# A gate piece moved into the attention, one unit's output products brought forward, and column halves at the end of a hybrid attention step

## The chip, the cores and the metric

The kernel runs on one core of one Trainium2 chip. The metric is the device time of one execution in microseconds (us), lower being better. Of the core's engines this text speaks of PE (TensorE, matrix products), DVE (VectorE), ACT (ScalarE), POOL (GpSimd) and SP (SyncE, which here only issues transfers, in order). Matrix products land in eight accumulation banks of 128 x 512 numbers; each engine works through its own instructions in the order of the program, and every bank or tile that is used again has to be read out first.

## The reference

One layer of a hybrid backbone on 128 context tokens and 1024 latent tokens of width 1024, all in 32-bit floats. The input is normalised and modulated, projected once, and split into queries, keys, values and gates of two mixers of 8 heads (2 key heads each, head width 64). Mixer A attends from every latent token to all 1152 keys, mixer B to a band of 128 to each side and the context keys, with a sink logit; the context tokens attend only to themselves. The outputs, each times the SiLU of its gate, go through one output projection, and are added to the input:

```python
def merge_out(o_a, g_a, o_b, g_b, w_out):
    return jnp.concatenate([o_a * jax.nn.silu(g_a), o_b * jax.nn.silu(g_b)], axis=-1) @ w_out

q_a, k_a, v_a, g_a, q_b, k_b, v_b, g_b = project(h, w_in[l], qn_a[l], kn_a[l], qn_b[l], kn_b[l])
...
o_a = global_attn_latent(q_a, k_a, v_a, cache_k_a[:, l], cache_v_a[:, l])
o_b = window_attn_latent(q_b, k_b, v_b, cache_k_b[:, l], cache_v_b[:, l], sink_b[l])
xs = xs + gate * merge_out(o_a, g_a, o_b, g_b, w_out[l])
```

## The kernel before

Most products are made of two or three: a number is split into a rounded high part and the low part that is left, and high x high, high x low and low x high go into one bank.

**Projections and gates** come first. The last of them are mixer B's gates (`gates`, a generator with one piece per turn): 512 gate columns in four groups `ch` of 128, tokens in three ranges (0 to 512, 512 to 768, 768 to 1152), so twelve pieces. A piece is 24 products into one bank (L259, L263, L264: eight weight slices, three products each; 128 x 384 for the last token range); a step later `put_gates` applies SiLU on ACT (L290, tile `sg`) and sends the result by SP to `g_dram` (`gd`), from which each attention unit loads its gate tile `sgl`. Beside the products of these pieces run the row maxima of attention units 0 and 2 (list `beside`, 26 items, spread evenly) and the splitting of `w_out` into its parts (`WO_STEPS`). Then comes one table load on ACT (L1074): after it exp and log are used, and the SiLU function no more.

**Attention** is a hand-written list of slots over 36 units (token tile t, mixer m, key head g): for t = 1 to 8 in turn (t,A,0), (t,B,0), (t,A,1), (t,B,1), the context tile's four units as the last ones (32 to 35). A unit of mixer A has 9 slots (blocks of 128 keys), one of mixer B 2 or 3, a context unit is padded to 2. Unit 0 has slots 0 to 8, unit 1 slots 9 to 11, unit 2 slots 12 to 20, unit 3 slots 21 to 23, unit 4 begins at 24. One turn of the main loop, one step, does in this order:

- `tick`: whatever earlier steps put off to this one (`later`).
- `scores` of the slot: mixer A: two products into a bank of pair B (L1125 with `qt`, L1126 with `qb`, which holds the negative row maxima; together `st`), exp on ACT (L1128, `pe`), the high part by an ACT cast (L1132, `ph`), the low part on POOL (L1136, on DVE for block 4; `pl`). Mixer B: four transposes of ready weights (L1120), an ACT copy (L1121, `ph`) and a subtraction on DVE a step later (L1122, `pl`).
- what is due at this step (`due`): the maxima of unit i are made during unit i-2 (`max_items`: PE L886 into a bank of pair A, tile `pmx`, DVE reduction L887, 12 each); `finish` closes them at step `start[i-2] + MX_END` = 10, and two steps later a transpose (L905, `ptm`) and a DVE product (L906) fill `qb`. Mixer B's weights (`weight_items`: scores `sn` L943 and L944, the masked minimum on DVE L947) are made in unit i-1.
- output products from the queue `outq`, 2.5 a step.
- `values` of the slot three steps back (LAG): L1146, L1148, L1149 into the unit's bank `pv` of pair C.

After a unit's last values: 1, 4 and 6 steps later (`END_AT`; for the context tile 2, 4, 5) ACT forms the reciprocal row sums from `pv` (`inverse`), DVE writes the quotient into the scratch tile `spare`, columns 768 to 1536, a third for each of three units (`gated`, L1170), POOL multiplies by the gate, and ACT and POOL split the result (`parts`, `ogh` and `ogl`). When a pair of units (A and B of one key head) is done, its 24 output products (`out_items`, `po`, L1217: two column halves n of 512, four slices of 128, three products each) enter `outq`; n = 0 goes to bank D and n = 1 to bank E. With the tile's last product DVE multiplies by the row `gate` (L1223), adds the input (L1224, `yt`) and SP sends the result.

**The last tile** (the context tokens) has its products in this order: two slices for both column halves, then the two other slices for both; at the end its second column half is read in two pieces of 256 columns. `spare` and the `gate` rows lie in tiles of the normalised input that the gates no longer need.

Of the kernel before, what the change touches and what calls it, by code (L numbers as in the profile page):

```python
# [9 lines left out]
F32 = mybir.dt.float32  # L10
# [8 lines left out]
P = 128  # L19
D = 1024  # L20
# [27 lines left out]
MX_END = 10  # L48
SPLIT_LAG = 2
# [32 lines left out]
AHEAD = 3  # L82

# [25 lines left out]
def hybrid_step(ctx, tc, x_prompt, x_sample, cache_k_a, cache_v_a, cache_k_b, cache_v_b,  # L109
# [749 lines left out]

    qp2 = []  # L860
# [194 lines left out]
    beside[:2] = 0.0, (len(beside[2]) + 0.5) / 64  # L1055
# [23 lines left out]
    spare = h_slot(1, 2, 4, "spare").bitcast(F32)  # L1079
    wo_big[2] = h_slot(1, 2, 0, "wo_big2")  # L1080
    gate = spare[:, 0:512], wo_big[2].bitcast(F32)[:, 1024:1536]
    for n in range(2):
        nc.sync.dma_start(gate[n], gate_row[0:1, 512 * n : 512 * n + 512].to_broadcast([P, 512]))
    ogp = ctx.enter_context(tc.tile_pool(name="ogp", bufs=NOG, side="right"))
    w2 = ctx.enter_context(tc.tile_pool(name="w2", bufs=2, side="right"))
    def blocks(t, m, g):
# [117 lines left out]
    def out_items(t, g):  # L1204
# [3 lines left out]
        def mm(n, k, p):  # L1208

            if k == KS[0] and p == 0:  # L1210
                po[n] = bank("DE"[n], f"po{t}_{n}")
# [5 lines left out]
            nc.tensor.matmul(po[n], a, wo_parts[KT * n + k][lo], start=(k == KS[0] and p == 0),  # L1217
                             stop=(k == KS[-1] and p == 2))
            if n == 1 and k % 2 == 1 and p == 2:
                held[0] -= 1  # L1220
            if k == KS[-1] and p == 2:
                for q in (slice(0, 256), slice(256, 512)) if last and n else (slice(0, 512),):
                    nc.vector.tensor_tensor(po[n][:, q], po[n][:, q], gt[n][:, q], op=ALU.mult)  # L1223
                    nc.vector.tensor_tensor(yt[n][:, q], po[n][:, q], yt[n][:, q], op=ALU.add)  # L1224
                    nc.sync.dma_start(y_tile[t][:, 512 * n + q.start : 512 * n + q.stop], yt[n][:, q])

        ks = KS[4 * g : 4 * g + 4]
        return [lambda n=n, k=k, p=p: mm(n, k, p)
# [122 lines left out]
```

## Time and profile before

| | before |
|---|---|
| time, median of 3 runs (lowest to highest) | 711.05 us (710.64 to 711.44) |
| the profiled execution: its time / its span | 710.47 / 708.7 us |
| mean granted PE clock in it | 0.997 |
| PE busy | 690.7 us, 97% |
| DVE busy | 469.8 us, 66% |
| ACT busy | 409.8 us, 58% |
| POOL busy | 335.3 us, 47% |
| read / written in memory | 58.69 / 19.18 MB |

The span is the traced part of one execution, in us from its start; times of the trace are such positions. A row of the timeline gives start, length, engine, line, operation, tiles (out<-in) and their size; a bracket [0.41 <-DVE spare L1170] says that the engine had stood idle for 0.41 us, and that DVE's instruction of line 1170 on `spare` ended this. PE's rows overlap (one begins while the one before drains), so that their price is the distance from start to start. The table of stages gives each engine's busy us and instructions in the order PE, its weight loads, DVE, ACT, POOL, and then the granted clock of PE, the busy share of the transfer engines and GB/s. The attention begins at about 302 us.

### The profile page before, as it was taken

Reading aid. Unit: us, or ns where it says so; the run is one execution under the profiler, and the core shown is the slowest. Engines: PE = TensorE matmul, PEld = TensorE weight load, DVE = VectorE, ACT = ScalarE, POOL = GpSimd, SP = SyncE. Lnnn points to the kernel's source line nnn. Section 1 sums busy time; section 2 is a strip of 40 time slices with the busy share of each in tenths; the row PEclk is TensorE's granted clock in tenths of the full one; section 3 lists DMA queues with packets and bytes.
Section 4 is the critical chain, followed back from the end, with each engine's and each line's share of the span. In section 5 each row is a group of like instructions: output and inputs, shape, how many; then the busy total and the mean of one; then the engine's idle time right before and its main releaser. Section 6 shows DMA issues by size and latency. Waiting matters only on the chain. (4 is left out here: it accounts for less than half of the span.)

```text
span 708.7 us, 10599 instructions
## 1 busy us (share of the span) xinstructions
PE 690.7 (97%) x3508; PEld 557.7 (79%) x3508; DVE 469.8 (66%) x1019; ACT 409.8 (58%) x829; POOL 335.3 (47%) x356
## 2 busy tenths in 40 slices
PE   6999999999999999999999999999999999999987
PEld 3778988878778889966788788888888888787865
DVE  4767257967868855637867578666775776675662
ACT  6646412412413431088777887788778777877760
POOL 4547033233223411256656655665576557555660
PEclk9999999999999999999999999999999999999999
DMA  8962273358353106432222121212221221222323
GB/s 324 414 216 92 78 302 75 89 158 260 104 125 99 46 31 216 130 100 63 73 68 87 48 83 53 73 55 75 68 82 39 79 70 54 74 74 68 104 68 120
DMA packets 53560, 78.58 MB, mean 111 GB/s; under 512 B 7096, under 2 KB 25720, under 8 KB 52608
## 3 DMA queue, kind: packets, MB, share of 16 engines
q1 hardware_dynamic: 45328, 65.96, 27.7%
q10 hardware_dynamic: 8176, 11.94, 6.3%
q8 instruction: 28, 0.46, 0.3%
q14 instruction: 28, 0.23, 0.1%
HBM read 58.69 MB, written 19.18 MB: 110 GB/s over the span
## 5 line engine op out<-in xcount | busy, mean ns | idle before, releaser
L1136 POOL TENSOR_TENSOR pl<-pe,ph 128x512 fp32r<-128x512 f32 x130 | 167.5, 1291 | 144.7 <-DVE nm L947 67.2
L887 DVE TENSOR_REDUCE mx<-pmx 128x1 f32<-128x384 f32 x192 | 101.3, 552 | 57.4 <-PE pmx L886 56.1
L1128 ACT ACTIVATE pe<-st 128x512 f32<-128x512 f32 x146 | 86.8, 594 | 28.0 <-PE st L1126 27.0
L1132 ACT CAST ph<-pe 128x512 fp32r<-128x512 f32 x146 | 90.6, 621 | 4.8
L1146 PE MATMUL pv<-ph,v_hi 128*128 128x512 f32 x208 | 83.5, 401 | 2.2 <-DVE spare L1170 2.2
L1149 PE MATMUL pv<-pl,v_hi 128*128 128x512 f32 x208 | 82.7, 398 | 0.0
L1217 PE MATMUL po<-wo,ogh 128*128 128x512 f32 x216 | 72.5, 394 | 0.2 <-DVE yt L1224 0.2
L174 POOL TENSOR_TENSOR rs_q<-ms_q,mhalf 128x8 f32<-128x8 f32 x18 | 34.1, 1897 | 80.9 <-DVE ms_q L172 80.9
L947 DVE CUSTOM_DVE_ANT_0 sn<-sn,mask,nsink 128x512 f32<-128x512 f32 (+1 forms) x64 | 46.4, 724 | 37.8 <-PE sn L944 36.7
L886 PE MATMUL pmx<-kha,qt 128*128 128x384 f32 x192 | 61.0, 363 | 0.4 <-DVE mx L887 0.2
L1125 PE MATMUL st<-qt,kha 128*128 128x512 f32 x144 | 58.0, 403 | 1.5 <-ACT pe L1128 0.8
L1126 PE MATMUL st<-qb,kla 68*128 68x512 f32 x144 | 57.5, 399 | 1.1 <-DVE qb L906 1.1
L1148 PE MATMUL pv<-ph,v_lo 128*64 128x512 f32 x146 | 57.9, 397 | 0.0
L1149 PEld LDWEIGHTS pv<-pl,v_hi 128*128 128x128 f32 x208 | 39.5, 190 | 16.9 <-POOL pl L1136 0.2
L933 ACT ACTIVATE pen<-sn,nm 128x512 f32<-128x512 f32 (+2 forms) x72 | 45.0, 626 | 6.5 <-DVE nm L947 3.1
L1121 ACT CAST ph<-st 128x512 fp32r<-128x512 f32 x62 | 36.4, 586 | 19.9 <-PE st L1120 18.2
L1146 PEld LDWEIGHTS pv<-ph,v_hi 128*128 128x128 f32 x208 | 39.3, 189 | 10.5 <-ACT ogh L1182 2.4
L1217 PEld LDWEIGHTS po<-wo,ogh 128*128 128x128 f32 x216 | 40.1, 188 | 6.8 <-DVE yt L1224 0.6
L646 ACT CAST qo0q<-ptq 128x512 fp32r<-128x512 f32 x18 | 10.6, 586 | 58.0 <-PE ptq L643 56.7
L1122 DVE TENSOR_TENSOR pl<-st,ph 128x512 fp32r<-128x512 f32 x62 | 42.5, 686 | 2.2 <-ACT ph L1121 1.5
L1217 PE MATMUL po<-wo,ogl 128*128 128x512 f32 x108 | 42.5, 394 | 0.0
L886 PEld LDWEIGHTS pmx<-kha,qt 128*128 128x128 f32 x192 | 35.5, 190 | 6.2 <-DVE mx L887 1.2
(213 smaller groups left out, 1696.9 us busy)
## 6 DMA issues: line engine op xcount, KB each, us to landing
qt<-qd SPq DMA_DIRECT2D x36, 256.0 KB, 3.0
wm<-in_w_mod_ss_dram SPq DMA_DIRECT2D x7, 1024.0 KB, 10.9
qd<-qo0q ACTq DMA_DIRECT2D x36, 128.0 KB, 2.4
qd<-qo1q ACTq DMA_DIRECT2D x36, 128.0 KB, 2.4
sgl<-gd SPq DMA_DIRECT2D x36, 128.0 KB, 2.2
out_dram<-yt SPq DMA_DIRECT2D x17, 256.0 KB, 2.0
xn<-in_x_sample_dram SPq DMA_DIRECT2D x8, 512.0 KB, 6.2
wg<-in_w_mod_g_dram SPq DMA_DIRECT2D x4, 1024.0 KB, 8.0
```

What stands on the lines that cost most here:

```text
L886: nc.tensor.matmul(pm[:, 0:384], lhs, kha[:, g, 3 * b : 3 * b + 3, :], start=True, stop=True)
L887: nc.vector.tensor_reduce(mx[:, h, b : b + 1], pm[:, 0:384], axis=AX.X, op=ALU.max)
L947: nc.vector.tensor_tensor_reduce(s, s, mask[:, m0 : m0 + n], -1.0, nsink[:, 4 * g + h : 4 * g + h + 1], op0=ALU.add, op1=ALU.min, accum_ou ...
L1125: nc.tensor.matmul(s, kh, qtile[i], start=True, stop=False)
L1126: nc.tensor.matmul(s, kl, qbtile[i], start=False, stop=True)
L1128: nc.scalar.activation(pe, s, AF.Exp)
L1132: nc.scalar.copy(ph, pe)
L1136: nc.gpsimd.tensor_tensor(pl, pe, ph, op=ALU.subtract)
L1146: nc.tensor.matmul(pv, two, ph, start=(b == 0), stop=False)
L1148: nc.tensor.matmul(pv[0:64, :], vl, ph, start=False, stop=False)
L1149: nc.tensor.matmul(pv, two, pl, start=False, stop=last)
L1217: nc.tensor.matmul(po[n], a, wo_parts[KT * n + k][lo], start=(k == KS[0] and p == 0), stop=(k == KS[-1] and p == 2))
```

## The change

**One gate piece is moved.** The last of mixer B's twelve pieces (`ch` 3, tokens 768 to 1152) is taken off the gate phase (`pieces.pop()`). ACT copies the 16 weight slices that it needs (high and low of eight) into tiles of the pool `ogp`, which is opened earlier for it (`hold`, one slice pair per half piece). Its 24 products are made in steps 0 to 3 of the attention, six a step, into bank D (`held_gates`, `pg_held`). SiLU is made from exp and log alone, since their table is in by then: for x, DVE copies x and max(x, -80) out of the bank into columns 768 to 1536 of `spare` (step 5, `held_exp`); ACT makes exp(-x), log(1 + that) and exp(-that) in place, 128 x 384 each, at steps 6, 7 and 8 (`held_steps`); POOL multiplies by x, and SP sends the piece to `g_dram`, at step 10 (`held_put`). `spare` lies on part of the normalised input that the held products still read, so it is opened, and the `gate` rows loaded, at step 5 (`open_spare`). The maxima of units 0 and 2 are spread over 56 groups of three products instead of 64.

**Unit 0's products early.** Unit 0 ends 1, 3 and 5 steps after its last values instead of 1, 4 and 6, and two steps after that, at step 18, its own 12 products of the first output (two of the four slices) enter the queue. The 12 of unit 1 follow when it is ready. Before, all 24 entered together after unit 1.

**Maxima closed earlier where the next unit is near.** `finish` comes at the smaller of `start[i-2] + 10` and `start[i] - 3`.

**The end.** The context units of mixer B take their value bank from pair A instead of C. The last tile's products are made with all slices of a column half in one go: first n = 0, whole, whose product with the gate row DVE writes to a tile `part` and POOL adds to the input; then n = 1 as two runs of 12 products of 256 columns, each in a bank of its own (E, and one of pair C), each read and sent by itself.

```diff
+MX_LEAD = 3
+HOLD_AT = 1
+HELD = (0, 0, 1, 1, 2, 2, 3, 3)
+HELD_END = (5, 6, 7, 8, 10)
+FIRST_END = (1, 3, 5, 7)
...
         pieces = [(ch, slice(a, b)) for a, b in thirds for ch in range(4)]
+        if m:
+            pieces.pop()
...
-    beside[:2] = 0.0, (len(beside[2]) + 0.5) / 64
+    beside[:2] = 0.0, (len(beside[2]) + 0.5) / 56
+    def hold(k):
+        w = ogp.tile([P, 2, P], F32R, tag="og" + "hl"[k % 2], name=f"held{k}")
+        for x, part in enumerate((W_GB.hi, W_GB.lo)):
+            nc.scalar.copy(w[:, x], part[k][:, 3 * P : 4 * P])
+        held_w.append(w)
+    for k in range(KT):
+        later(HOLD_AT + k, lambda k=k: hold(k))
...
+    def held_gates(k):
+        i, to = third(last_piece)
+        if k == 0:
+            gl["pg"] = bank("D", "pg_held")[:, 0:LN]
+        w = held_w[k]
+        for x, y in ((0, 0), (1, 0), (0, 1)):
+            nc.tensor.matmul(gl["pg"], w[:, x], h_at(y, i, k, to), start=(k == 0 and x == 0 and y == 0),
+                             stop=(k == KT - 1 and y == 1))
+    def held_exp():
+        gl["x"], gl["e"] = spare[:, 768 : 768 + LN], spare[:, 768 + LN : 768 + 2 * LN]
+        nc.vector.tensor_copy(gl["x"], gl["pg"])
+        nc.vector.tensor_scalar(gl["e"], gl["pg"], -80.0, None, op0=ALU.max)
+    def held_put():
+        nc.gpsimd.tensor_tensor(gl["x"], gl["x"], gl["e"], op=ALU.mult)
+        nc.sync.dma_start(g_dram[TOP : TOP + P, last_piece], gl["x"])
+    held_steps = [held_exp,
+                  lambda: nc.scalar.activation(gl["e"], gl["e"], AF.Exp, scale=-1.0),
+                  lambda: nc.scalar.activation(gl["e"], gl["e"], AF.Ln, bias=1.0),
+                  lambda: nc.scalar.activation(gl["e"], gl["e"], AF.Exp, scale=-1.0),
+                  held_put]
...
-            pvb[i] = bank("C", f"pv{i}")
+            pvb[i] = bank("C" if t or m == 0 else "A", f"pv{i}")
...
-        ends = END_AT if t else PROMPT_END
+        ends = FIRST_END if i == 0 else END_AT if t else PROMPT_END
+        if i == 0:
+            later(ends[3], lambda: outq.extend(out_items(t, g, 1)))
         if m == 1:
-            later(ends[3], lambda: outq.extend(out_items(t, g)))
+            later(ends[3], lambda: outq.extend(out_items(t, g, 2 if i == 1 else 3)))
...
+        def done(n, q):
+            if last and n == 0:
+                part = w3.tile([P, 512], F32, tag="pe", name=f"part{t}", bufs=PES)
+                nc.vector.tensor_tensor(part, po[n, 0], gt[n], op=ALU.mult)
+                nc.gpsimd.tensor_tensor(yt[n], part, yt[n], op=ALU.add)
+            else:
+                s = po[n, q.start]
+                nc.vector.tensor_tensor(s, s, gt[n][:, q], op=ALU.mult)
+                nc.vector.tensor_tensor(yt[n][:, q], s, yt[n][:, q], op=ALU.add)
+            nc.sync.dma_start(y_tile[t][:, 512 * n + q.start : 512 * n + q.stop], yt[n][:, q])
+        ks = KS[4 * g : 4 * g + 4][2 * (half == 2) : 4 - 2 * (half == 1)]
+        whole, halves = (slice(0, 512),), (slice(0, 256), slice(256, 512))
+        out = []
+        for n in range(2):
+            out += [lambda n=n, k=k, p=p, q=q: mm(n, k, p, q)
+                    for q in (halves if last and n else whole) for k in ks for p in range(3)]
...
-            at, end = [start[i - 2] + a for a in (MX_AT if i > 2 else MX_FIRST)], start[i - 2] + MX_END
+            at, end = [start[i - 2] + a for a in (MX_AT if i > 2 else MX_FIRST)], min(start[i - 2] + MX_END, start[i] - MX_LEAD)
...
+    for k, at in enumerate(HELD):
+        put(at, lambda k=k: held_gates(k))
+    put(HELD_END[0], open_spare)
+    for f, at in zip(held_steps, HELD_END):
+        put(at, f)
```

The numbers at the ends of tile names below only tell copies apart. PE at the beginning of the attention, before: the last transposed maxima (`ptm`), the scores of blocks 0 and 1 (`st_0`, `st_1`) and unit 1's weights (`sn`).

```order
L905 MATMUL ptm_3375<-ident_r,m_nat_109 4x128
L1125 MATMUL st_0_3378<-qt_2962,kha 128x512
L1126 MATMUL st_0_3378<-qb_3154,kla 128x512
L943 MATMUL sn_0_3392<-khb,qt_2964 128x384
L944 MATMUL sn_0_3392<-klb,qt_2964 128x384
L1125 MATMUL st_1_3397<-qt_2962,kha 128x512
L1126 MATMUL st_1_3397<-qb_3154,kla 128x512
```

The same place after.

```order
L913 MATMUL ptm_3367<-ident_r,m_nat_109 4x128
L1181 MATMUL st_0_3370<-qt_2965,kha 128x512
L1182 MATMUL st_0_3370<-qb_3160,kla 128x512
L951 MATMUL sn_0_3384<-khb,qt_2967 128x384
L952 MATMUL sn_0_3384<-klb,qt_2967 128x384
L1122 MATMUL pg_held<-h_2_0_139,held_2985 128x384 x2
L1122 MATMUL pg_held<-h_2_0_141,held_2985 128x384
L1122 MATMUL pg_held<-h_2_0_139,held_3005 128x384 x2
L1122 MATMUL pg_held<-h_2_0_141,held_3005 128x384
L1181 MATMUL st_1_3396<-qt_2965,kha 128x512
L1182 MATMUL st_1_3396<-qb_3160,kla 128x512
```

Six products of the held piece now stand behind each of the scores 0 to 3.

ACT at the end of unit 0 (blocks 6 to 8 of mixer A, then unit 1's blocks 0 and 1), before.

```order
L1128 ACTIVATE pe_6_3477<-st_6_3472 128x512
L1132 CAST ph_6_3473<-pe_6_3477 128x512
L1128 ACTIVATE pe_7_3489<-st_7_3484 128x512
L1132 CAST ph_7_3485<-pe_7_3489 128x512
L1128 ACTIVATE pe_8_3501<-st_8_3496 128x512
L1132 CAST ph_8_3497<-pe_8_3501 128x512
L1121 CAST ph_0_3516<-st_0_3515 128x512
L999 COPY spare<-pti_3531 4x128
L1121 CAST ph_1_3537<-st_1_3536 128x512
```

After.

```order
L1184 ACTIVATE pe_6_3500<-st_6_3495 128x512
L1188 CAST ph_6_3496<-pe_6_3500 128x512
L1137 ACTIVATE spare<-spare 128x384
L1184 ACTIVATE pe_7_3513<-st_7_3508 128x512
L1188 CAST ph_7_3509<-pe_7_3513 128x512
L1138 ACTIVATE spare<-spare 128x384
L1184 ACTIVATE pe_8_3526<-st_8_3521 128x512
L1188 CAST ph_8_3522<-pe_8_3526 128x512
L1139 ACTIVATE spare<-spare 128x384
L1177 CAST ph_0_3542<-st_0_3541 128x512
L1007 COPY spare<-pti_3557 4x128
L1177 CAST ph_1_3563<-st_1_3562 128x512
```

The three functions of the held piece stand between the casts of blocks 6, 7 and 8 and the next scores' reading.

PE's last products, before: `po_0` is the context tile's first column half, `po_1` its second.

```order
L1217 MATMUL po_1_8123<-wo_11_3831,ogl_8079 128x512
L1217 MATMUL po_0_8116<-wo_6_3211,ogh_8103 128x512
L1217 MATMUL po_0_8116<-wo_6_3212,ogh_8103 128x512
L1217 MATMUL po_0_8116<-wo_6_3211,ogl_8104 128x512
L1217 MATMUL po_0_8116<-wo_7_3236,ogh_8103 128x512
L1217 MATMUL po_0_8116<-wo_7_3237,ogh_8103 128x512
L1217 MATMUL po_0_8116<-wo_7_3236,ogl_8104 128x512
L1217 MATMUL po_1_8123<-wo_big_3553,ogh_8103 128x512
L1217 MATMUL po_1_8123<-wo_big_3362,ogh_8103 128x512
```

After, around the last change of bank (`po_1_0` is the second half's first 256 columns, `po_1_256` the rest).

```order
L1275 MATMUL po_1_0_8157<-wo_big_3582,ogh_8131 128x256
L1275 MATMUL po_1_0_8157<-wo_big_3485,ogh_8131 128x256
L1275 MATMUL po_1_0_8157<-wo_big_3582,ogl_8132 128x256
L1275 MATMUL po_1_256_8170<-wo_10_3363,ogh_8106 128x256
L1275 MATMUL po_1_256_8170<-wo_10_3364,ogh_8106 128x256
L1275 MATMUL po_1_256_8170<-wo_10_3363,ogl_8107 128x256
L1275 MATMUL po_1_256_8170<-wo_11_3876,ogh_8106 128x256
```

The two column halves took turns by slices before; after, the last 12 products all belong to the last 256 columns.

More of the change, by code (lines that the diff above doesn't have):

```diff
@@ L858, in hybrid_step @@
     penat = {}
+    ogp = ctx.enter_context(tc.tile_pool(name="ogp", bufs=NOG, side="right"))
     qp2 = []
@@ L1078, in hybrid_step, with open_spare @@
     w3 = ctx.enter_context(tc.tile_pool(name="w3", bufs=4, side="right"))
[L1079 to L1084, printed above, removed]
-    w2 = ctx.enter_context(tc.tile_pool(name="w2", bufs=2, side="right"))
+    w2 = ctx.enter_context(tc.tile_pool(name="w2", bufs=2, side="right"))
+    spare, gate = None, []
+    def open_spare():
+        nonlocal spare
+        spare = h_slot(1, 2, 4, "spare").bitcast(F32)
+        wo_big[2] = h_slot(1, 2, 0, "wo_big2")
+        gate.extend((spare[:, 0:512], wo_big[2].bitcast(F32)[:, 1024:1536]))
+        for n in range(2):
+            nc.sync.dma_start(gate[n], gate_row[0:1, 512 * n : 512 * n + 512].to_broadcast([P, 512]))
+    last_piece = slice(*THIRDS[2])
+    LN = last_piece.stop - last_piece.start
+    gl = {}
+    def held_gates(k):
[13 more added lines that the diff above has]
+        nc.sync.dma_start(g_dram[TOP : TOP + P, last_piece], gl["x"])
+    TOP = 512 + 3 * P
+    held_steps = [held_exp,
[3 more added lines that the diff above has]
+                  held_put]
     def blocks(t, m, g):
@@ L1202, in load_sum, with out_items, mm @@
             nc.sync.dma_start(gt[n], gate_row[1:2, hs].to_broadcast([P, 512]))
-    def out_items(t, g):
+    def out_items(t, g, half):
         last = t == units[-1][0]
-        def mm(n, k, p):
+        def mm(n, k, p, q):
             if k == KS[0] and p == 0:
-                po[n] = bank("DE"[n], f"po{t}_{n}")
+                po[n, q.start] = bank("C" if q.start else "DE"[n], f"po{t}_{n}_{q.start}")[:, 0 : q.stop - q.start]
             if n == 0 and k == KS[4] and p == 0:
@@ L1216, in mm @@
             a, lo = ((oh, 0), (oh, 1), (ol, 0))[p]
-            nc.tensor.matmul(po[n], a, wo_parts[KT * n + k][lo], start=(k == KS[0] and p == 0),
+            nc.tensor.matmul(po[n, q.start], a, wo_parts[KT * n + k][lo][:, q], start=(k == KS[0] and p == 0),
                              stop=(k == KS[-1] and p == 2))
-            if n == 1 and k % 2 == 1 and p == 2:
+            if n == 1 and k % 2 == 1 and p == 2 and q.stop == 512:
                 held[0] -= 1
             if k == KS[-1] and p == 2:
[L1222 to L1228, printed above, removed]
-                for kk in ((ks[:2], ks[2:]) if last else (ks,)) for n in range(2) for k in kk for p in range(3)]
+                done(n, q)
+        def done(n, q):
[11 more added lines that the diff above has]
+        out = []
+        for n in range(2):
+            out += [lambda n=n, k=k, p=p, q=q: mm(n, k, p, q)
+                    for q in (halves if last and n else whole) for k in ks for p in range(3)]
+        return out
     slots, start = [], []
```

1 line of the change is left out of this document (added).

## The prediction

> **What bounds the kernel now.** The page's first line says which engine sets the time.
>
> ```profile
> PE 690.7 (97%) x3508; PEld 557.7 (79%) x3508; DVE 469.8 (66%) x1019; ACT 409.8 (58%) x829; POOL 335.3 (47%) x356
> ```
>
> So I read PE's waits next: what it waits for is all that a reordering can give back. Two that recur in the attention (engine, what waited, what released it: total us, times, longest):
>
> ```profile
> PE pv L1146 <- DVE spare L1170: 2.2, 4, 1.0
> PE st L1126 <- DVE qb L906: 1.1, 2, 0.6
> ```
>
> Then the table by stage, to see where they lie (us of each engine, then PE's granted clock, DMA share, GB/s).
>
> ```profile
> 305.00:310.00 5.00, 4.03 (x13) 2.55 (x12) 1.37 (x4) 4.91 (x13) 3.83 (x3) 0.80 0.86 277
> 325.00:330.00 5.00, 4.41 (x20) 3.00 (x19) 2.54 (x7) 4.89 (x13) 4.45 (x5) 1.00 0.01 2
> 360.00:380.00 20.00, 20.00 (x99) 16.10 (x98) 14.21 (x30) 15.37 (x31) 10.63 (x11) 1.00 0.24 72
> ```
>
> In the attention's first steps, before 330, ACT is busy throughout and PE is not; at 360 PE has no hole, and a microsecond comes off there only with PE work. So the change can win in three places: the first steps, the two units after them, and the last 30 us.
>
> **First steps: the moved gate piece.** The timeline of PE and ACT from the last gate product to unit 1's first transposes (start, length):
>
> ```profile
> 301.91 0.23 PE L905 MATMUL ptm<-ident_r,m_nat 128*4 128x128 f32 x1
> ...
> 308.02 0.63 PE L1146 MATMUL pv<-ph,v_hi 128*128 128x512 f32 x1
> ...
> 311.42 0.39 PE L1125 MATMUL st<-qt,kha 128*128 128x512 f32 x1
> 311.65 0.39 PE L1126 MATMUL st<-qb,kla 68*128 68x512 f32 x1
> ...
> 316.24 0.60 PE L1120 MATMUL st<-ident_r,pen 128*128 128x128 f32 x4
> ```
>
> ```profile
> 298.61 0.33 PE L263 MATMUL pg<-h,whigb 128*128 128x384 f32 x1
> 298.78 0.34 PE L264 MATMUL pg<-h,wlogb 128*128 128x384 f32 x1
> ```
>
> A 512-column product takes 0.23 us from start to start, a 384-column one 0.17. From 301.91 to 316.24, 14.33 us, PE has 18 score and 18 value products (8.3), 8 of 384 columns (1.4) and 0.2 of small ones: 9.9 us. 4.4 us are lost. Of these 1.6 are a slow stretch: the 8 products from 308.02 to 311.42 take 0.425 each instead of 0.23. The rest are waits for ACT.
>
> Removed in front are 24 products of 0.17: the attention starts 4.2 us earlier. The same 24 come back six to a step in steps 0 to 3, so step 0 to unit 1's transposes holds 9.9 + 4.2 = 14.1 us of PE work. If PE never waits, the transposes come at 297.7 + 14.1 = 311.8, a gain of 4.4: the upper bound. Against it stands ACT:
>
> ```profile
> 302.16 0.49 ACT L290 ACTIVATE sg<-pg 128x384 f32<-128x384 f32 x1 [4.21 <-PE ptm L905]
> 302.67 1.28 ACT L1074 ACT_TABLE_LOAD   x1
> 303.97 0.60 ACT L1128 ACTIVATE pe<-st 128x512 f32<-128x512 f32 x1
> ...
> 305.69 0.59 ACT L1128 ACTIVATE pe<-st 128x512 f32<-128x512 f32 x1
> ...
> 316.88 0.59 ACT L1121 CAST ph<-st 128x512 fp32r<-128x512 f32 x1
> ```
>
> The last gate SiLU and the table load behind it move ahead by the same 4.2, so the first exponential starts at 299.8. Steps 0 to 3 take 1.72 of ACT each; PE now needs 0.46 + 0.35 + 1.04 = 1.85, so PE sets the pace, and it is dense: I take the slow stretch to go. In steps 4 to 8 ACT has an exponential and a cast a step, 0.59 each by their rows and a little less from start to start, an estimate of 1.15; PE has 1.15 too, and ACT now gets three more instructions of 128x384, priced like the SiLU row at 0.49: 1.4 us that PE's pace does not leave room for. Counting ACT from 299.8: 4 x 1.72, 5 x 1.15, 0.2 and 1.4 give 314.0 for unit 1's first cast, 2.9 earlier than 316.88 and not 4.4. What follows it is a chain on DVE, and PE's first scores of unit 2 behind it:
>
> ```profile
> 317.53 0.68 DVE L1122 TENSOR_TENSOR pl<-st,ph 128x512 fp32r<-128x512 f32 x1
> 318.47 1.02 DVE L887 TENSOR_REDUCE mx<-pmx 128x1 f32<-128x384 f32 x2 [0.27 <-PE pmx L886]
> ...
> 320.47 0.68 DVE L1122 TENSOR_TENSOR pl<-st,ph 128x512 fp32r<-128x512 f32 x1
> ```
>
> ```profile
> 321.30 0.47 PE L1125 MATMUL st<-qt,kha 128*128 128x512 f32 x1 [0.69 <-DVE pl L1122]
> ```
>
> The scores wait for the second subtraction. DVE itself waited 0.3 us here for PE's maxima, which will now be there in time. So unit 2 starts some 3.2 us earlier, and a little more if an activation's start-to-start time is under its length, as it is for the score rows; I take **-3.4**, from -2.4 (another microsecond of ACT) to -4.4. The 16 extra ACT copies of weights lie under the gate products, where ACT does little; two DVE reads of the held bank, a POOL product and its DMA lie where those engines wait for ACT's casts. The DMA waits on SP for that product, and behind it stand unit 0's row sums and loads of later units, not the next step's. These cost nothing unless the cover goes; then each costs its own length, the copies least, as the gate products have time.
>
> The 26 items of the early maxima are spread over 56 groups of three products, not 64. Each maximum needs half a microsecond of DVE (two took 1.02 at 318.47) before its bank comes free, and a weight split that lay under the last piece falls into step 0. With a maximum a microsecond DVE has room on average but not in bunches: **+0.2**, from 0 to +0.8.
>
> **Unit 0's output products early.** 12 products of 0.23, 2.8 us, move from unit 4 into unit 2 and 3's steps. PE's holes there:
>
> ```profile
> 326.73 0.48 PE L1146 MATMUL pv<-ph,v_hi 128*128 128x512 f32 x1 [0.41 <-DVE spare L1170]
> ...
> 335.15 0.44 PE L886 MATMUL pmx<-kha,qt 128*128 128x384 f32 x1 [0.19 <-DVE mx L887]
> ...
> 342.13 0.50 PE L1126 MATMUL st<-qb,kla 68*128 68x512 f32 x1 [0.64 <-DVE qb L906]
> ```
>
> A hole is some 0.2 longer from start to start than the wait in brackets (the pair of rows below shows 0.7 for 0.49), so these come to 0.6, 0.4 and 0.8; with smaller ones I estimate 2.4. The first goes as unit 0 is gated a step earlier, the third as unit 4's maximum is closed a slot earlier (12 slots between the units, so 9 instead of 10), and the products fill the second. But ACT at 4.9 of 5 us is the limit until 330, so PE running ahead waits again; and unit 4's later steps lose the cover of the products. 2.4 at most, 0.3 at least; I take **-1.3**, nearer the wait that surely goes (0.8) than all of them. The earlier closing helps once more, at unit 30:
>
> ```profile
> 649.50 0.44 PE L1125 MATMUL st<-qt,kha 128*128 128x512 f32 x1
> 650.43 0.50 PE L1126 MATMUL st<-qb,kla 68*128 68x512 f32 x1 [0.49 <-DVE qb L906]
> ```
>
> 0.93 from start to start instead of 0.23: **-0.6** (0.3 to 0.7).
>
> **The end.** Value products of the prompt's units 33 and 35 wait until a bank of pair C is read; they move to pair A.
>
> ```profile
> 681.15 0.39 PE L1217 MATMUL po<-wo_big,ogh 128*128 128x512 f32 x1
> 682.50 0.47 PE L1146 MATMUL pv<-ph,v_hi 128*128 128x512 f32 x1 [0.96 <-DVE spare L1170]
> ...
> 685.21 0.40 PE L1149 MATMUL pv<-pl,v_hi 128*128 128x512 f32 x1
> 686.29 0.47 PE L1146 MATMUL pv<-ph,v_hi 128*128 128x512 f32 x1 [0.69 <-DVE spare L1170]
> ```
>
> ```profile
> 684.55 0.69 DVE L1122 TENSOR_TENSOR pl<-st,ph 128x512 fp32r<-128x512 f32 x1
> ```
>
> 1.1 and 0.85 us go as waits. Late next is unit 35's own data: its second part is subtracted on DVE until 685.24, behind ACT's reciprocal of unit 32, and no bank changes that. So its second value product starts at 685.3, and not 0.3 behind the row at 686.29: **-1.3** (0.5 to 2.0). Then the prompt's products:
>
> ```profile
> 693.44 0.39 PE L1217 MATMUL po<-wo,ogl 128*128 128x512 f32 x1
> ...
> 693.99 0.73 PE L1217 MATMUL po<-wo,ogh 128*128 128x512 f32 x2 [0.16 <-DVE yt L1224]
> ...
> 703.41 0.39 PE L1217 MATMUL po<-wo_big,ogl 128*128 128x512 f32 x1
> ```
>
> With all 12 products of the left half first, the right half's bank is read in time: 0.55 instead of 0.23 from start to start, **-0.3**. At the very end stand four DVE instructions, from the last product's bank to the output:
>
> ```profile
> 703.84 0.43 DVE L1223 TENSOR_TENSOR po<-po,gt 128x256 f32<-128x256 f32 x1
> ...
> 705.23 0.42 DVE L1224 TENSOR_TENSOR yt<-po,yt 128x256 f32<-128x256 f32 x1
> ```
>
> The first two now run under the last 12 products: 2 x 0.46 = 0.9 less. For that 24 products of 512 become 48 of 256, priced by the gates:
>
> ```profile
> 279.73 0.28 PE L264 MATMUL pg<-h,wlogb 128*128 128x256 f32 x1
> 279.85 0.28 PE L259 MATMUL pg<-h,whigb 128*128 128x256 f32 x1
> ```
>
> 48 x 0.12 - 24 x 0.23 = 0.2 more. **-0.7** (0.5 to 0.8). The left half's extra POOL sum has the 24 narrow products, 2.8 us, as cover.
>
> **The sum.** -3.4 + 0.2 - 1.3 - 0.6 - 1.3 - 0.3 - 0.7 = -7.4 against the profiled execution's 710.47 us (span 708.7 and 1.8 around it): 703.1. The median of the runs shown lies 0.6 above that execution, so the forecast is 703.7. The terms' ends add up to -3.4 and -11; all at one end is unlikely.
>
> **Rivals.** (1) *The slow stretch stays.* For: PE was busy 4.03 of 5 us around it, so waits need not be its cause. Against: it lies in the stretch with most waits, and at 325 to 330, with 4.41, and at 360 the clock is 1.00. The gain is 1.6 smaller, 705.3. The Trainium skill, TensorE: Matmul & The Clock Gate, section HAM oscillation, says that the clock halves after idle gaps longer than about 3.4 us; by that rule these short gaps would not cause the drop, and filling them would not remove it: 705.3. The trace shows a drop without such a gap, so the rule does not hold for this one as it stands. Chance 0.1. (2) *ACT eats the start.* The three functions stop the chain longer than 1.4, or a weight split blocks the first maxima: the start gives 2.0, 705.1, with PE's longer wait at unit 2's first scores. Chance 0.17. (3) *The early products only move the holes*: PE waits as long in units 2 to 4 as before, 705.0. Chance 0.15. (4) *Slower: the held piece's transfer stops DVE.* The held product lies in the columns of `spare` where unit 0's gated output goes; DVE, in order, must wait for that transfer to land before it writes. Transfers of this size in the gates' stretch (KB, median us to landing):
>
> ```profile
> gd<-sg SPq DMA_DIRECT2D x3, 192.0 KB, 3.1
> ```
>
> It is issued some 2 us after ACT's third function, near 316; DVE comes to the write about 321 (the row at 326.73, less its own two instructions, a step and 3.4), 5 later. Each microsecond beyond stops DVE, and with it scores and values; from 12.4 on the whole 7.4 is gone, and at 15 the time is 713.7. Chance 0.03. (5) *The change does not do what it says at the end*: the halves' transfers set it and not DVE, so the 0.9 stays and the narrow products cost 0.2: 704.6. Chance 0.05. The forecast keeps 0.5.
>
> **The numbers.** A measurement here can tell 0.2%, 1.4 us. Only (4) ends above 711; two rivals together, 706.6, still end faster. Faster 0.95, same 0.02, slower 0.03. The range takes in each rival alone and two of them together with 0.6 between runs, 707.2, and of the terms' better ends, 3.6 together, 2.5: 701.2 to 707.2.
>
> **What would show it.** Right: no stretch of the first steps with a clock under 1; unit 1's first transposes about 312; no wait of values for the gated output after 680; one pair of DVE instructions behind the last product. Wrong: a PE wait of over 2 us at unit 2's first scores, new waits in unit 4, or DVE waiting for a transfer in unit 2.

## The result and the profile after

The changed kernel took 705.76 us (median of 5 runs, 705.33 to 706.16), against 711.05 us before (5 runs, 710.59 to 711.73). The ratio is 0.9924, with a 95% interval of 0.9913 to 0.9934, so that the change takes off 5.4 us, 4.7 to 6.2. The forecast was 703.7 and its range 701.2 to 707.2. The time lies in that range; one cost of the prediction's sum was too small, and two of its gains were too large. The profiled execution took 706.05 us with a span of 704.3, 4.4 less than the span before.

The first line of the page after, and PE's waits (engine, what waited, what released it: total us, times, longest):

```profile
PE 689.0 (98%) x3532; PEld 557.9 (79%) x3532; DVE 469.2 (67%) x1020; ACT 412.9 (59%) x847; POOL 337.5 (48%) x358
```

```profile
PE st L1181 <- DVE pl L1178: 0.8, 1, 0.8
PE ptm L913 <- DVE mx L895: 0.8, 1, 0.8
PE pmx L894 <- ACT pen L941: 0.6, 1, 0.6
PE pv L1205 <- DVE pl L1178: 0.5, 1, 0.5
PE pmx L894 <- DVE mx L895: 0.5, 1, 0.5
...
PE pv L1202 <- DVE spare L1226: 0.2, 1, 0.2
```

The two kinds of wait that the prediction began with are gone or nearly so: values for the gated output from 2.2 to 0.2, scores for `qb` from 1.1 to none. In their place stand new ones: the transposed maxima in the gate phase (0.8), the maxima's products in units 2 and 3 (for ACT's weights `pen` 0.6 and for DVE's `mx` 0.5, 0.2 each before), and a value product at the end that waits for DVE's subtraction `pl` (0.5). Unit 2's first scores had waited 0.7 for `pl` before, and wait 0.8 now.

The table by stage for the first steps (columns as before) shows that the slow stretch went: 0.80 and 0.86 were the clocks here.

```profile
305.00:310.00 5.00, 5.00 (x25) 4.17 (x24) 1.39 (x4) 4.87 (x12) 3.19 (x4) 1.00 0.75 194
310.00:315.00 5.00, 5.00 (x28) 3.85 (x27) 2.12 (x5) 4.90 (x11) 4.11 (x5) 1.00 0.37 123
```

Since most of the program is the same before and after, the same instruction can be looked up in both timelines. These marks say where the 4.4 us were made:

| start on PE of | before | after | difference |
|---|---|---|---|
| mixer B's first gate product | 246.09 | 246.43 | +0.34 |
| unit 2's transposed maxima (`ptm`), just ahead of the attention | 301.91 | 299.07 | -2.84 |
| unit 1's first transposes | 316.24 | 313.31 | -2.93 |
| unit 2's first scores | 321.30 | 319.15 | -2.15 |
| unit 6's first scores | 366.54 | 363.89 | -2.65 |
| unit 28's first scores | 628.59 | 626.24 | -2.35 |
| unit 30's second scores | 652.29 | 649.36 | -2.93 |
| unit 34's scores | 679.54 | 676.62 | -2.92 |
| end of the last DVE instruction | 705.65 | 701.26 | -4.39 |

The first row is no work of the change: the first inputs came 0.34 later in this execution. So unit 2's first scores stand 2.5 better by the change's own doing. Rows of the timeline after, on PE: two `ptm`, then the scores of unit 2.

```profile
284.65 0.22 PE L913 MATMUL ptm<-ident_r,m_nat 128*4 128x128 f32 x1 [0.80 <-DVE mx L895]
...
299.07 0.23 PE L913 MATMUL ptm<-ident_r,m_nat 128*4 128x128 f32 x1
...
319.15 0.47 PE L1181 MATMUL st<-qt,kha 128*128 128x512 f32 x1 [0.82 <-DVE pl L1178]
```

And ACT around unit 1's first casts:

```profile
314.70 0.52 ACT L1139 ACTIVATE spare<-spare 128x384 f32<-128x384 f32 x1
315.13 0.57 ACT L1177 CAST ph<-st 128x512 fp32r<-128x512 f32 x1
...
315.75 0.57 ACT L1177 CAST ph<-st 128x512 fp32r<-128x512 f32 x1
317.55 0.59 ACT L1177 CAST ph<-st 128x512 fp32r<-128x512 f32 x1 [1.23 <-PE st L1176]
```

PE had unit 1's transposes done at 313.9, and ACT read them only at 315.13, behind the last function of the held piece. The price of one, 0.43 from start to start, is near the 0.49 that was taken.

PE at the end, from the context's last value products on, and the chain that ended last (start, length, what):

```profile
681.39 0.50 PE L1202 MATMUL pv<-ph,v_hi 128*128 128x512 f32 x1
682.38 0.50 PE L1205 MATMUL pv<-pl,v_hi 128*128 128x512 f32 x1 [0.49 <-DVE pl L1178]
...
684.12 0.62 PE L1275 MATMUL po<-wo,ogh 128*128 128x512 f32 x2
684.86 0.50 PE L1275 MATMUL po<-wo,ogl 128*128 128x512 f32 x1
```

```profile
683.36 0.74 POOL spare L1228
684.10 0.71 POOL ogl L1240
684.81 0.04 issue
684.86 3.92 PE po L1275 x16
688.77 0.07 issue
688.84 11.51 PE po L1275 x72
```

The waits for the gated output are gone, and `pl` is late next, as forecast. But then two more things are late that had not been: the low part `ogl` on POOL at 684.86 (0.28 more than the usual 0.46 from the row ahead, and 0.1 behind it), and bank D, read by DVE, at 688.84 (0.2 and 0.1 more). The two cost about 0.7.

The last DVE instructions:

```profile
697.50 0.69 DVE L1286 TENSOR_TENSOR part<-po,gt 128x512 f32<-128x512 f32 x1 [7.26 <-PE po L1275]
...
700.37 0.43 DVE L1290 TENSOR_TENSOR po<-po,gt 128x256 f32<-128x256 f32 x1 [0.54 <-PE po L1275]
700.84 0.42 DVE L1291 TENSOR_TENSOR yt<-po,yt 128x256 f32<-128x256 f32 x1
```

One pair follows the last product, which starts at 700.05, and DVE ends 1.2 behind that start and not 2.2 (703.41 to 705.65 before).

### The profile page after: what moved, and what is told of

Its sections match the earlier page's. It is cut to its first block, busy times and chain, and to the rows that moved or that the text cites. A ratio compares the mean times of both kernels' runs of the same rounds, so it can differ in the third digit from the quotient of the medians.

```text
span 704.3 us, 10666 instructions
## 1 busy us (share of the span) xinstructions
PE 689.0 (98%) x3532; PEld 557.9 (79%) x3532; DVE 469.2 (67%) x1020; ACT 412.9 (59%) x847; POOL 337.5 (48%) x358
## 5 line engine op out<-in xcount | busy, mean ns | idle before, releaser
L1275 PE MATMUL po<-wo,ogh 128*128 128x512 f32 (+1 forms) x224 | 73.1, 387 | 0.1
L653 ACT CAST qo0q<-ptq 128x512 fp32r<-128x512 f32 x18 | 10.6, 586 | 58.3 <-PE ptq L650 57.0
L1275 PE MATMUL po<-wo,ogl 128*128 128x512 f32 (+1 forms) x112 | 43.4, 387 | 0.1
```

The costliest lines, as they stand in the source:

```text
L1275: nc.tensor.matmul(po[n, q.start], a, wo_parts[KT * n + k][lo][:, q], start=(k == KS[0] and p == 0), stop=(k == KS[-1] and p == 2))
```

## The experiments

Twelve runs followed, in four groups, each group on one chip beside the kernel before; that took 711.19, 711.07, 711.29 and 710.77 us there. Ratios are to it. Differences under 0.7 us are inside the spread of the runs, so such terms are read from marks, counted from an earlier mark of the same execution.

**The gate piece alone.** Undone:

```diff
-        if m:
-            pieces.pop()
...
-    beside[:2] = 0.0, (len(beside[2]) + 0.5) / 56
+    beside[:2] = 0.0, (len(beside[2]) + 0.5) / 64
...
-    for k, at in enumerate(HELD):
-        put(at, lambda k=k: held_gates(k))
```

> The held gate piece goes back among the gate products (maxima spread over 64 groups again), all else stays as in the changed kernel. Theory, from the marks of the two traces: the moved piece is worth the 2.5 us by which unit 2's first scores came earlier (the 4.15 of its products, less 0.96 lost in the gate phase and 0.7 up to unit 2), so 705.8 + 2.5 = 708.3 us, and a stretch with a granted clock under 1.00 comes back in the first attention steps. Rival, the clock's drop has nothing to do with PE's waits there: the stretch stays at 1.00. Second rival, what the piece gains is given back in units 2 to 4: under 707.0.

709.06 us, ratio 0.9969 (0.9957 to 0.9981), so that the piece is worth 3.2 us by the times. By the marks it is worth 2.5: unit 2's first scores come 75.27 us behind mixer B's first gate product, and 72.72 in the changed kernel. The slow stretch is back at its old place (table by stage of this kernel):

```profile
305.00:310.00 5.00, 4.03 (x13) 2.60 (x12) 1.37 (x4) 4.91 (x13) 3.84 (x3) 0.77 0.86 286
310.00:315.00 5.00, 5.00 (x21) 3.74 (x20) 0.69 (x1) 4.82 (x11) 3.01 (x5) 0.89 0.03 13
```

The other 0.7 lie between unit 4's and unit 6's first scores (22.71 us here, 22.01 in the changed kernel). In unit 4's steps of this execution PE waits for the gated output, and the rows of POOL, DVE and PE show why:

```profile
348.73 1.29 POOL L1190 TENSOR_TENSOR pl<-pe,ph 128x512 fp32r<-128x512 f32 x1 [0.52 <-ACT ph L1186]
```

```profile
348.76 1.55 DVE L1048 CAST wo_big<-wraw 128x512 fp32r<-128x512 f32 x1 [0.90 <-DMA wraw<-in_w_out_dram]
...
351.89 0.47 PE L1200 MATMUL pv<-ph,v_hi 128*128 128x512 f32 x1 [0.46 <-DVE spare L1224]
```

A cast of `w_out` began 0.03 behind POOL's subtraction and took 1.55 us, where the changed kernel's trace has 0.43 (at 346.19), and DVE's quotient came late by it. The last section has more of this kind. Whether it belongs to this kernel or to this execution, one trace does not show. A second measurement of the changed kernel, which had a loss of that kind too, is told below; beside its ratio of 0.9934 the piece is worth 2.5 by the times as well. So the first rival and the second are out, and the theory's 2.5 holds; its 708.3 was 0.8 short.

**Do the held products cost anything in steps 0 to 3?** Only 3 of the 24 are made (the other 21 are left out):

```diff
+        if k:
+            return
         w = held_w[k]
...
-                             stop=(k == KT - 1 and y == 1))
+                             stop=(y == 1))
```

> The changed kernel with 3 of the 24 held products (left out: the 21 others, 3.6 us of PE work in steps 0 to 3; ACT, DVE and POOL do all that they did). Theory: the held products lie wholly under ACT's pace of 1.72 a step, and without them PE stands there and its clock falls: unit 1's transposes within 0.4 of the changed kernel's, a granted clock under 1.00 again between 304 and 312, time within 0.4. Rival, PE sets the pace of the first steps: unit 1's transposes 1 us or more earlier, clock 1.00.

706.25 us, ratio 0.9928 (0.9916 to 0.9941). From `ptm` to unit 2's first scores it took 20.01 us, and 20.08 in the changed kernel: 21 products cost 0.07. Unit 1's first transposes came 0.75 earlier (13.49 behind `ptm` and not 14.24), outside the theory's 0.4 and short of the rival's 1 us; but ACT read them at 15.98 and not 16.06, so that PE's lead was of no use. ACT sets the pace, as the theory said: in the changed kernel its exponentials of blocks 0 to 3 start at 301.12, 302.84, 304.56 and 306.27, 1.72 apart. The theory's other half failed: the clock stayed at 1.00, with PE busy 3.74 of the 5 us from 300. Between step 1's and the first value products PE was busy 2.58 of 3.84 us; before the change it was 2.59 of 4.36. So the next run moved the 3 products out of that stretch:

```diff
-HELD = (0, 0, 1, 1, 2, 2, 3, 3)
+HELD = (4, 4, 4, 4, 4, 4, 4, 4)
```

> The run before with 3 of the 24 held products (21 left out) kept its granted clock at 1.00 with PE busy 2.6 of the 3.8 us from its step 1 to its first values; here its 3 products stand behind step 4's scores, so that PE has in steps 0 to 3 just what it had before the change. Theory: the halved clock belongs to how empty PE is there (busy 2.6 of 4.4 us before the change, 2.3 of 4.1 with the piece put back), so it comes back: a granted clock of 0.5 for about 3 us between 304 and 310. Rival, the moved piece's copies, loads or the earlier start kept it away: clock 1.00. The time within 0.5 of that run, 706.2, by ACT's pace.

706.03 us, ratio 0.9930 (0.9916 to 0.9944). The stage table, in steps of 1 us:

```profile
304.00:305.00 1.00, 0.52 (x2) 0.29 (x2) 0.46 (x2) 1.00 (x4) 0.83 (x1) 0.88 0.97 239
305.00:306.00 1.00, 1.00 (x4) 0.80 (x4) 0.14 (x1) 0.97 (x3) 0.57 (x2) 0.50 0.97 201
...
308.00:309.00 1.00, 1.00 (x6) 0.86 (x5) 0.00 (x0) 0.97 (x3) 1.00 (x2) 0.91 0.00 0
```

The half clock is back, for 3.4 us (three full rows, and 0.24 and 0.18 by the first and the last), and unit 2's first scores come 20.74 behind `ptm`, 0.7 later than with it at 1.00. Between these two traces, three products more or less just ahead of the emptiest stretch make the difference: the drop belongs to how empty PE is there. Where the limit lies stays open: there was a drop with PE busy 2.59 of 4.36 us, and none with 2.58 of 3.84.

Nor does the program alone decide it. One execution of each kernel has a trace; of the others the mean granted clock is known, and it says that the drop comes and goes. The traced execution of the kernel before, with its one drop, has 0.997. Of that kernel's 44 executions beside these experiments, 16 have 0.999 or 1.000 and took 710.7 us on average; 26 have 0.996 or less and took 711.5. All ten executions of the changed kernel have 0.999 or 1.000. Of the run with 3 products in step 0 it is four of five, of this one one of five. So the products change how often the drop comes.

**ACT's three functions** are left out (the SiLU of one gate piece):

```diff
-    held_steps = [held_exp,
-                  lambda: nc.scalar.activation(gl["e"], gl["e"], AF.Exp, scale=-1.0),
-                  lambda: nc.scalar.activation(gl["e"], gl["e"], AF.Ln, bias=1.0),
-                  lambda: nc.scalar.activation(gl["e"], gl["e"], AF.Exp, scale=-1.0),
+    held_steps = [held_exp, lambda: None, lambda: None, lambda: None,
```

> The changed kernel without ACT's three functions of the held piece (left out: the SiLU of one gate piece; DVE's reads, POOL's product and the transfer stay). Theory, the prediction's: ACT is what holds unit 1's casts, so unit 1's first cast comes 1.2 to 1.4 us earlier, unit 2's first scores 0.7 earlier, and the time is 0.7 under the changed kernel's, 705.8 against 706.5 on the chip of the run before. Rival, unit 2's scores hang on DVE's subtractions and PE's maxima and not on ACT: under 0.2 earlier.

705.73 us, ratio 0.9925 (0.9912 to 0.9939). Unit 1's first cast:

```profile
313.53 0.59 ACT L1174 CAST ph<-st 128x512 fp32r<-128x512 f32 x1
```

That is 14.88 behind `ptm` at 298.65, and 16.06 in the changed kernel: 1.2 earlier. Unit 2's first scores come 19.35 behind it and not 20.08, 0.7 earlier, as the theory had it, and unit 6's keep that.

**Unit 0's products** back in their old place:

```diff
-        ends = FIRST_END if i == 0 else END_AT if t else PROMPT_END
+        ends = END_AT if t else PROMPT_END
...
-        if i == 0:
-            later(ends[3], lambda: outq.extend(out_items(t, g, 1)))
...
-            later(ends[3], lambda: outq.extend(out_items(t, g, 2 if i == 1 else 3)))
+            later(ends[3], lambda: outq.extend(out_items(t, g, 3)))
```

> Unit 0's end and its 12 output products go back to their old places, all else stays, the earlier closing of unit 4's maxima too. Theory: the early products filled few holes, and by unit 5 nothing of them is left; within 0.3 of the changed kernel, 705.8. Rival, as the prediction's term had it without the unit-4 wait: 0.5 to 1.0 slower, 706.3 to 706.8, with a wait of values for the gated output back in unit 3's steps.

705.70 us, ratio 0.9918 (0.9903 to 0.9933). From unit 2's to unit 6's first scores it gained 0.67 on the kernel before (-2.12 to -2.79), and the whole change 0.50: the early products cost 0.17. The wait for the gated output is back,

```profile
PE pv L1202 <- DVE spare L1226: 0.6, 2, 0.4
```

and the two of the changed kernel in units 2 and 3 (0.61 for ACT's weights, 0.48 for DVE's maxima) are shorter, 0.2 each.

**The earlier closing of the maxima** undone:

```diff
-            at, end = [start[i - 2] + a for a in (MX_AT if i > 2 else MX_FIRST)], min(start[i - 2] + MX_END, start[i] - MX_LEAD)
+            at, end = [start[i - 2] + a for a in (MX_AT if i > 2 else MX_FIRST)], start[i - 2] + MX_END
```

> Only the earlier closing of the maxima of units 4 and 30 is undone. Theory: it is what gained in units 2 to 4, with or without the early products; PE's waits for qb come back, 0.6 to 0.8 at unit 4's first scores and 0.5 at unit 30's, each 0.6 to 0.8 on the path: 707.0. Rival, by the time of unit 4 the early products cover the wait: only unit 30's comes back, 706.4.

707.46 us, ratio 0.9952 (0.9939 to 0.9964); the changed kernel on the same chip took 706.48. Both waits are back:

```profile
PE st L1182 <- DVE qb L914: 1.0, 2, 0.5
```

Unit 4's second scores come 45.49 us behind unit 2's `ptm`, and 44.67 in the changed kernel; unit 30's come 2.79 behind its first scores, and 2.06 there. The rival is out: each is worth 0.7 to 0.8.

**The context's value banks** back in pair C:

```diff
-            pvb[i] = bank("C" if t or m == 0 else "A", f"pv{i}")
+            pvb[i] = bank("C", f"pv{i}")
```

> Only the value banks of the context's mixer-B units go back to pair C. Theory: the waits of 1.1 and 0.85 us for the gated output come back and the two new ones (0.4 for POOL's low part, 0.3 at bank D) go, so the change of banks is worth 0.5 and not the 1.3 of the prediction: 706.3, and 0.5 more from unit 32's scores to the last product. Rival, the prediction's term: the new waits have another cause and stay, 707.1, with 1.2 more in that stretch.

706.77 us, ratio 0.9941 (0.9928 to 0.9953), beside 706.48. PE's rows:

```profile
679.69 0.47 PE L1202 MATMUL pv<-ph,v_hi 128*128 128x512 f32 x1 [0.96 <-DVE spare L1226]
...
683.48 0.47 PE L1202 MATMUL pv<-ph,v_hi 128*128 128x512 f32 x1 [0.69 <-DVE spare L1226]
```

Both old waits are back, and from there to the end no distance from start to start is longer than usual: the waits for `ogl` and for bank D are gone. From unit 34's scores to the last product it took 23.86 us, and 23.43 in the changed kernel. The banks are worth 0.4.

**The last tile** in its old order and width:

```diff
...
-        out = []
-        for n in range(2):
-            out += [lambda n=n, k=k, p=p, q=q: mm(n, k, p, q)
-                    for q in (halves if last and n else whole) for k in ks for p in range(3)]
-        return out
+        return [lambda n=n, k=k, p=p: mm(n, k, p, whole[0])
+                for kk in ((ks[:2], ks[2:]) if last else (ks,)) for n in range(2) for k in kk for p in range(3)]
```

> The last tile's products go back to the old order and width (two slices for both column halves, then the other two; no 256-column products, no sum on POOL), the value banks stay in pair A. Theory: the new order gains 0.9 at the last DVE instructions and 0.3 at bank E, and loses 0.3 to narrow products and some 0.7 to new waits (for POOL's low part and for DVE's reading of bank D), so that going back costs only 0.2: 706.0. Rival, the prediction's terms hold and the new waits have another cause that stays: 1.0 slower, 706.8.

707.02 us, ratio 0.9936 (0.9922 to 0.9950). From unit 34's scores (676.17) to DVE's end

```profile
701.08 0.42 DVE L1286 TENSOR_TENSOR yt<-po,yt 128x256 f32<-128x256 f32 x1
```

it took 25.33 us, and 24.64 in the changed kernel: order and halves together are worth 0.7. The theory's 0.2 fell, because the waits for `ogl` and bank D are in this kernel too, as the rival had it; they come with the value banks, which let PE run ahead into them. The rival's 1.0 fell as well: the wait at bank E, which the new order was to remove, is 0.1 in this kernel and not the 0.3 of the kernel before, since PE comes to that bank later by the wait at bank D.

**What the losses cost, and a better kernel.** Unit 0's transposed maxima one step later:

```diff
-            later(TURN, transpose)
+            later(TURN + (i == 0), transpose)
```

> Only unit 0's transposed maxima are read by PE one step (12 gate products, 2 us) later, so that PE needn't stand still for DVE there. Theory: the 0.8 us wait of the denser maxima goes and nothing takes its place, 705.0, with the attention's first scores 0.8 earlier. Rival, DVE as a whole is late: the wait comes back at the next maxima or at unit 2's transposed maxima, 705.8.

```profile
286.12 0.22 PE L913 MATMUL ptm<-ident_r,m_nat 128*4 128x128 f32 x1
...
298.11 0.23 PE L913 MATMUL ptm<-ident_r,m_nat 128*4 128x128 f32 x1
```

The wait is gone, and 0.95 with it (unit 2's `ptm` comes 51.69 behind mixer B's first gate product, and 52.64 in the changed kernel), all of it kept to unit 34. 705.37 us, ratio 0.9916 (0.9900 to 0.9931): the mean gain is smaller than the runs' spread, and the marks carry it.

The changed kernel again:

> The changed kernel itself, once more on this chip, as the measure for the others: 705.8. Every theory expects the same marks as in its first trace, 0.96 lost in the gate phase, up to the arrival of the first inputs and a pace in the attention that differed by up to 0.5 us over 260 us between executions.

706.48 us, ratio 0.9934 (0.9921 to 0.9948). Its marks agree to 0.1 with those of its first trace up to unit 4, and then it lost 0.65 at one place, told in the last section. On this chip the change takes off 4.6 us.

Then four edits together (the one above, unit 0's products late, the low parts at once, and the last tile's left half in another bank):

```diff
-            later(1, lambda: nc.gpsimd.tensor_tensor(ol, v["of"], oh, op=ALU.subtract))
...
+            low = lambda: nc.gpsimd.tensor_tensor(ol, v["of"], oh, op=ALU.subtract)
+            if i < NU - 5:
+                later(1, low)
+            else:
+                low()
...
+                po[n, q.start] = bank("C" if q.start else "B" if last and n == 0 else "DE"[n], f"po{t}_{n}_{q.start}")[:, 0 : q.stop - q.start]
```

> The changed kernel with four edits: unit 0's transposed maxima one step later, unit 0's output products back in their old place, the low parts of units 31 to 35 made on POOL at once and not a step later, and the last tile's first column half in a bank of pair B (free by then) instead of D. Theory: 0.96 in the gate phase, 0.2 in units 2 to 4 and the two waits of 0.4 and 0.3 at the end go: 705.8 - 1.8 = 704.0, seen at the marks. Rival, what is late next takes the end's 0.7: 704.7.

704.24 us, ratio 0.9905 (0.9892 to 0.9919), beside 706.48: both waits of the end are gone (22.65 from unit 34's scores to the last product, and not 23.43). The marks give 0.95 in the gate phase, 0.2 in units 2 to 4 and 0.8 at the end, as the theory had it; the loss of 0.65 of the last section is in the trace beside it and not in this one, so that the 2.2 between the two times is more than the edits' own. And with ACT's functions later:

```diff
-HELD_END = (5, 6, 7, 8, 10)
+HELD_END = (5, 8, 9, 10, 11)
```

> The kernel of four edits (704.24 on its chip) with ACT's three functions at steps 8, 9 and 10 and not 6, 7 and 8, and POOL's product and its transfer at step 11. Theory: ACT waits for PE in unit 1's steps and has room there: unit 2's first scores 0.5 earlier, 703.7. Rival, the prediction's slower case: the transfer of the held piece lands too late for unit 0's quotient on DVE, DVE waits there, and scores and values behind it: slower than 704.7.

703.94 us, ratio 0.9899 (0.9886 to 0.9913). Unit 2's first scores come 19.99 behind `ptm`, and 20.08 in the kernel of four edits: 0.1 and not 0.5. Unit 1's first cast is 0.8 earlier, but PE's wait for `pl` is

```profile
PE st L1181 <- DVE pl L1178: 1.1, 1, 1.1
```

since a weight split stood ahead of that subtraction on DVE and took 1.38 us, 0.69 elsewhere. It came earlier here, and began while POOL made its product of the held piece; in the kernel of four edits that product was done 0.6 ahead of the split. The rows of DVE and POOL:

```profile
315.58 1.38 DVE L1051 TENSOR_TENSOR wo_big<-wraw,wo_big 128x512 fp32r<-128x512 f32 x1
```

```profile
315.16 1.26 POOL L1131 TENSOR_TENSOR spare<-spare 128x384 f32<-128x384 f32 x1 [0.82 <-ACT spare L1139]
```

DVE's quotient of unit 0, which has to wait for the held piece's transfer, has no wait in its row (no bracket):

```profile
322.15 0.84 DVE L1226 TENSOR_TENSOR spare<-pv,rs 64x256 f32<-64x256 f32 x2
```

The prediction's slower case did not come. The transfer is a step later here, but so is unit 0's quotient, which is back in its old place, so that the room between them is much the same; in the changed kernel too the quotient's row (322.21) has no bracket.

## Why the prediction came out as it did

**First steps: right in kind, one term mis-sized.** That the attention's first steps take in 4.2 us of products, that the slow stretch goes, that ACT gives back some of it and that the first cast comes 2.9 earlier, all this held (the cast: 316.88 to 315.13, and 0.34 of late inputs and 0.96 of the gate phase in it: 3.05). The step that failed is the price of the denser maxima, "**+0.2**, from 0 to +0.8": they cost 0.96. DVE's time was counted on average, and its price put on the banks of the maxima. What happened is a wait in order: PE's transposition of unit 0's maxima stands two half pieces behind their closing, wherever DVE is by then, and DVE had a weight split and the first of two reductions to finish before the bank came free for it at 284.65:

```profile
283.43 0.69 DVE L1051 TENSOR_TENSOR wo<-wraw,wo 128x512 fp32r<-128x512 f32 x1
284.04 1.02 DVE L895 TENSOR_REDUCE mx<-pmx 128x1 f32<-128x384 f32 x2
```

One step's delay of that transposition removes the whole loss. So the start gave 2.5 at unit 2's first scores and not 3.2; with the 0.96 put back it is 3.45, and the term of -3.4 stands. One reading in it was wrong and cost nothing: the prediction had PE set the pace of steps 0 to 3 with 1.85 a step, and ACT set it with 1.72; the sum had counted ACT.

**Units 2 to 4: rival (3) was right about the products.** The prediction valued unit 0's early products with the closing of unit 4's maxima at 1.3, "nearer the wait that surely goes (0.8) than all of them". Only that wait went, 0.8 by its own experiment (45.49 to 44.67); the products moved the holes and cost 0.17, so that the whole gave 0.5. This is the second mis-sized term. ACT was busy 4.85 of the 5 us from 325, and 4.89 before, and PE ahead of it waits somewhere else: 0.61 for ACT's weights in unit 2. The row that said so was quoted in the prediction's first part.

**Unit 30** gave 0.6, as forecast.

**The end.** The bank change gained 1.2 at the context's value products and gave 0.7 back at two waits that lay behind them, `ogl` on POOL and bank D on DVE. The prediction had named what is late next for value products and stopped there; it did not follow PE into the output products, where an earlier PE meets POOL and DVE that have not become earlier. At the place that it named it was right: unit 35's second value product comes 5.76 behind unit 34's scores, and 7.06 before, the 1.3 of the term. This is the third mis-sized term: -1.3, measured -0.4. Order and halves of the last tile were forecast at -0.3 and -0.7. With the old value banks they give 1.04 together (26.11 us from unit 34's scores to DVE's end before, 25.07 in the run of the value banks), with the new ones 0.7, since bank D's wait then stands in place of bank E's. Rival (5) is out.

**The sum.** By marks -2.5 - 0.5 - 0.6 - 1.5 (the whole end, 26.11 to 24.64 from unit 34's scores to DVE's end) make -5.1. Of the rest to -4.4, 0.34 are the late inputs and 0.3 a slower pace between units 6 and 28, both the execution's own. By medians it is -5.3. The ends of the prediction's terms add up to -3.5 and -10.6, and not to -3.4 and -11; nothing hangs on that.

**Rivals (1), (2) and (4).** The slow stretch went with the emptiness of PE and came back with it in the traces of two kernels, though not in each of their executions. The Trainium skill, page TensorE: Matmul & The Clock Gate, section HAM oscillation, has the clock fall after idle gaps of more than about 3.4 us. Here no single gap was over 1 us, so the measurement decides: short gaps are enough. The same page, in its Part 1, tells of an activity window of that length that runs freely; the 3.4 us for which the half clock lasted agree with that, though no run here shows the window itself. ACT's three functions cost 1.2 at unit 1's first cast, and 1.4 was forecast. The transfer of the held piece stopped nothing.

## What to carry to other kernels

Work moved into steps that another engine paces was free there (21 products cost 0.07 us), and made the drop of the clock rarer besides; but look at what the emptied place does to the engines that worked beside it. When a wait is removed, follow the engine that now runs ahead through the next two or three things it reads, not only the next one: POOL and DVE were late by 0.4 and 0.3 behind a gain of 1.2. Early work did not fill the holes of PE where it waits for ACT, which is busy throughout. And one trace can hold a loss of 0.7 us that another execution of the same kernel has not, so a difference of that size is followed to its row before it is put down to an edit.

## What the runs showed of the hardware that was not expected

The same small DVE instruction (128 x 4 numbers) took 0.17 us in one execution of the changed kernel and 1.33 us at the same place in another. The rows of DVE and POOL, first execution:

```profile
359.41 0.17 DVE L908 TENSOR_SCALAR m_nat<-m 128x4 fp32r<-128x4 f32 x1
```

```profile
359.50 1.27 POOL L1192 TENSOR_TENSOR pl<-pe,ph 128x512 fp32r<-128x512 f32 x1
```

Second execution:

```profile
359.51 1.33 DVE L908 TENSOR_SCALAR m_nat<-m 128x4 fp32r<-128x4 f32 x1
```

```profile
359.52 1.29 POOL L1192 TENSOR_TENSOR pl<-pe,ph 128x512 fp32r<-128x512 f32 x1
```

Where DVE came 0.1 ahead of POOL, it was done at once; where both came together, DVE ended 0.03 after POOL's instruction did. PE, which waits there for DVE's maxima, lost 0.65 us by it. The runs of the value banks and of 3 held products in step 0 have the same at this place (1.34 and 1.32). The Trainium skill, page SBUF — State Buffer, section SBUF: two separate sides, says that GpSimd and DVE, in some kinds of its instructions, share a pair of ports as an exclusive lock that whoever starts first holds for the whole instruction. The first execution agrees. In the second DVE's row begins 0.01 ahead of POOL's and DVE waits all the same, so that rows this close do not tell who was first. In the gate phase of the changed kernel the same instruction stood behind unit 0's maxima beside a weight split on POOL. DVE and POOL there:

```profile
282.33 0.74 DVE L908 TENSOR_SCALAR m_nat<-m 128x4 fp32r<-128x4 f32 x1
```

```profile
281.76 1.29 POOL L1051 TENSOR_TENSOR wo<-wraw,wo 128x512 fp32r<-128x512 f32 x1 [2.58 <-PE pmx L894]
```

It had taken 0.17 there before the change (283.76, on the kernel before), so that some 0.6 of the 0.96 that PE lost may come from this; that share was not measured by itself. The cast of 1.55 us in the first experiment and the split of 1.38 in the last, both begun during an instruction of POOL, fit the same cause; no run shows it for them.

The pace of the attention differs between executions by up to 0.2%: from unit 6's to unit 28's first scores, where all kernels issue the same instructions, it took 262.05 us before, 262.35 after, and between 262.05 and 262.53 in the other kernels, with a granted clock of 1.00 throughout. The cause stays open.
